# A hybrid attention and Mamba-2 layer on one core: the order of TensorE's work is written out by hand instead of left to the scheduler

## The chip, the core and the metric

The kernel runs on one core of a Trainium2 chip. The metric is the time of one execution on the device, in microseconds. The kernel is written in a tile language: the program names tiles, pools of buffers and instructions, and a scheduler puts the instructions of each engine into a queue. Each engine (TensorE or PE, VectorE or DVE, ScalarE or ACT, GpSimd or POOL, and SyncE or SP, which only starts DMAs) then runs its queue strictly in order, and waits at an instruction until its operands and its output buffer are free.

## What is computed

One decoder layer over 1024 tokens of width 1024, all in float32:

```python
h = rmsnorm(x, g_pre)
q, k, v, g_att, z, xbc, dt_raw, merge_logits = split(h @ w_in)
# branch A, 8 heads: two causal softmax maps a head, their difference
a = softmax(q0 k0' + bias) - lam * softmax(q1 k1' + bias)
o = rmsnorm(a @ v, att_subln_g) * (1 - lambda_init) * silu(g_att)
y_att = o @ w_att_proj
# branch B, 8 groups of 4 heads: Mamba-2 scan in chunks
xs, B, C = split(silu(causal_depthwise_conv(xbc)))
y = (ssd_chunked_scan(xs, softplus(dt), A, B, C) + xs * d_skip) * silu(z)
y_ssm = group_rmsnorm(y) @ w_ssm_proj
mixed = sigmoid(gate_att) * y_att + sigmoid(gate_ssm) * y_ssm
out = x + rmsnorm(mixed @ w_out, g_post)
```

## The kernel before

**Products.** Each large product is made of three: both operands are split into a high and a low part (`split`: ACT copies the high part, then DVE or POOL subtracts), and PE adds high x high, high x low and low x high (`mm3`, L144). A `proj_T` is half of a projection with transposed output: 24 matmuls of 512 columns. A `proj_N` is one block of 128 tokens: 24 matmuls of 256 columns.

**Stages.** First x is normalised and transposed into hTH and hTL. Then `attention(h)` runs for eight heads, with the projections of the merge gates (`gates`) behind each; then `branch_att` projects the attention output; then `ssm(g)` runs for eight groups, and the last four gates; then the last stage projects the ssm output (tiles pys), mixes, and makes the output projection (pout). Between stages the data go through DRAM: o_d, y_d, sig_d (gates), mix_d.

**In a head.** Projections pq, pk (two halves each) and pv (eight blocks, values and the output gate). Then, for each of eight blocks of 128 queries, `attend`: the scores s on PE; max, exponential and difference p on DVE and ACT; the transposes pta of p on PE and their split into ah and al; and the product po on PE. After four blocks, a part, comes the normalisation: ACT sums the squares of o, DVE computes the inverse root in ten small steps (`rsqrt`, `rms`), DVE scales the four tiles o, and PE transposes them (pto, L306). ACT evicts pto to oT, and a DMA writes it to o_d.

**In a group.** Projections pub, puc, pux (each with a convolution of four taps on DVE) and pz. Then, for each of eight chunks of 128 tokens, `prepare` (transposes px and a product on PE, several steps on ACT, DVE and POOL that make xb, xe, xdt, v, mt) and `advance` (the products pd on PE, the state st, the output v). After four chunks, a part, `finish` normalises as in attention: Square on ACT, the small DVE steps, four scalings of v, and the transposes pty (L627), which ACT evicts to yT, and which a DMA writes to y_d.

**What sets the order.** The program writes one head after the other and one group after the other. The scheduler decides for every engine, PE among them, which instruction goes next; it can move a later projection's matmuls in front of a transpose that isn't ready. Loads are issued from SP's queue. The stores sig_d, o_d, y_d and mix_d, the copies of kh and kl and the loads of mt are issued from ACT's queue. The low parts of the weights are made by DVE, except those of the gates and of the first head, which POOL makes.

**Buffers.** PSUM has three pools of two buffers: projections (`psp`), scores and pd (`pss`), and all else (`pst`: pta, po, pto, px, pty). The weights of one `proj_T` have two buffers.

## Time and profile before

| | |
|---|---|
| three runs | 1926.62, 1930.2, 1932.01 us; median 1930.2 |
| profiled execution | 1931.15 us, of which the span is 1929.4 us |
| granted TensorE clock over the span | 0.989 |
| PE busy | 1828.1 us (95%) |
| DVE, ACT, POOL busy | 1183.5, 862.4, 136.3 us |
| stages by their PE work | head to 52 us, attention to 712, its projection to 850, ssm to 1621, gates to 1641, last stage to the end |

A row of the timeline gives start, length, engine, line and names; in brackets stands the idle time of the engine before it and what ended that. A row of windows gives for each engine its busy time and, in parentheses, its instructions, then the granted clock of TensorE (PEclk, 1.00 is full speed), the share of the DMA engines and their rate. A row of the wait table gives the waiting instruction, what released it, the total, the number of waits, and the longest.

### The profile page before, as it was taken

The numbers are of one execution on the slowest core, as the hardware profiler recorded it, in microseconds if no ns is written. First come the engines' busy times: TensorE is split into PE (matmuls) and PEld (weight loads), VectorE is DVE, ScalarE is ACT, GpSimd is POOL, SyncE is SP. The second block draws the span as 40 slices with busy tenths as digits, with TensorE's granted clock in tenths as the row PEclk, the third lists the DMA queues.
The fourth block names the chain that finished last, engine by engine and source line by source line (L and its number), as shares of the span: only waits on it lengthen the run. The fifth ranks groups of instructions, "written<-read, shape, count | busy, mean of one in ns | idle before, by whom it ended". The sixth has DMA issues, their size and how long they took to land. (4 is left out here: it accounts for less than half of the span.)

```text
span 1929.4 us, 27946 instructions
## 1 busy us (share of the span) xinstructions
PE 1828.1 (95%) x10249; PEld 1564.5 (81%) x10249; DVE 1183.5 (61%) x2782; ACT 862.4 (45%) x2135; POOL 136.3 (7%) x154
## 2 busy tenths in 40 slices
PE   6999999999999999999899989998989999999998
PEld 4888889789888878888787878787878777877786
DVE  5576486766757553247576767676757676545433
ACT  6455364545636442125445444545444545332221
POOL 1000000000000010001010101010101022000000
PEclk9999999999999999999999999999999999999999
DMA  6121222222122135513222222222222225653532
GB/s 204 55 75 56 53 58 59 70 61 60 54 54 66 37 125 178 166 34 79 70 61 72 63 69 63 70 65 71 63 64 64 69 50 173 220 172 134 175 110 71
DMA packets 222279, 169.34 MB, mean 88 GB/s; under 512 B 12733, under 2 KB 187167, under 8 KB 222143
## 3 DMA queue, kind: packets, MB, share of 16 engines
q1 hardware_dynamic: 169390, 117.21, 20.7%
q10 hardware_dynamic: 52752, 50.36, 9.0%
q8 instruction: 81, 1.33, 0.3%
q14 instruction: 56, 0.45, 0.1%
HBM read 129.63 MB, written 31.08 MB: 83 GB/s over the span
## 5 line engine op out<-in xcount | busy, mean ns | idle before, releaser
L150 PE MATMUL pz<-wzh,hTL 128*128 128x256 f32 (+1 forms) x512 | 152.0, 297 | 0.0
L150 PE MATMUL pz<-wzh,hTH 128*128 128x256 f32 (+1 forms) x512 | 149.6, 292 | 0.3 <-DVE dtr L539 0.3
L150 PE MATMUL pz<-wzl,hTH 128*128 128x256 f32 (+1 forms) x512 | 148.0, 289 | 0.0
L150 PE MATMUL pv<-wvh,hTH 128*128 128x256 f32 x512 | 144.5, 282 | 0.7 <-DVE kl L277 0.4
L150 PE MATMUL pv<-wvl,hTH 128*128 128x256 f32 x512 | 144.8, 283 | 0.0
L150 PE MATMUL pv<-wvh,hTL 128*128 128x256 f32 x512 | 144.0, 281 | 0.0
L586 ACT ACTIVATE mt<-mt,acs 128x128 f32<-128x128 f32 x256 | 85.6, 391 | 112.9 <-DMA mt<-arow_d 112.9
L580 POOL TENSOR_TENSOR v<-xb,dsk 128x256 f32<-128x256 f32 x64 | 51.1, 808 | 683.6 <-ACT xb L572 613.6
L331 DVE TENSOR_REDUCE ng<-s 128x2 f32<-128x1024 f32 (+2 forms) x96 | 91.3, 952 | 12.4 <-PE s L323 11.9
L150 PEld LDWEIGHTS pv<-wvh,hTH 128*128 128x128 f32 x512 | 97.0, 190 | 2.3 <-PE pv L150 0.5
L150 PEld LDWEIGHTS pz<-wzh,hTH 128*128 128x128 f32 x512 | 97.7, 191 | 1.5 <-PE pz L150 0.5
L150 PEld LDWEIGHTS pz<-wzl,hTH 128*128 128x128 f32 x512 | 97.6, 191 | 0.5
L150 PEld LDWEIGHTS pz<-wzh,hTL 128*128 128x128 f32 x512 | 97.1, 190 | 0.7
L150 PEld LDWEIGHTS pv<-wvl,hTH 128*128 128x128 f32 x512 | 96.7, 189 | 0.3
L150 PEld LDWEIGHTS pv<-wvh,hTL 128*128 128x128 f32 x512 | 96.2, 188 | 0.0
L342 ACT ACTIVATE p<-s,ngm 128x512 f32<-128x512 f32 (+3 forms) x128 | 76.7, 610 | 34.9 <-DVE ngm L337 34.8
L513 DVE SCALAR_TENSOR_TENSOR xT<-ux,cw,xT 128x512 f32<-128x512 f32 x96 | 75.7, 789 | 20.2 <-ACT xT L511 18.8
L607 PE MATMUL pd<-xdt,mt 128*128 128x64 f32 x512 | 66.6, 273 | 11.0 <-DVE st L605 4.8
L607 PEld LDWEIGHTS pd<-xdt,mt 128*128 128x128 f32 x512 | 62.4, 191 | 16.4 <-ACT mt L586 9.0
L366 PE MATMUL po<-vv,ah 128*128 128x256 f32 x288 | 74.8, 289 | 0.0
L289 DVE TENSOR_TENSOR vv<-pv,vv 128x128 fp32r<-128x128 f32 x64 | 18.6, 291 | 87.8 <-ACT vv L288 87.6
L367 PE MATMUL po<-vv,al 128*128 128x256 f32 x288 | 71.8, 282 | 0.0
(869 smaller groups left out, 5423.0 us busy)
## 6 DMA issues: line engine op xcount, KB each, us to landing
mt<-arow_d ACTq DMA_DIRECT2D x64, 256.0 KB, 4.9
sig_d<-gt ACTq DMA_DIRECT2D x32, 256.0 KB, 2.1
y_d<-yT ACTq DMA_DIRECT2D x32, 256.0 KB, 2.1
yT_l<-y_d SPq DMA_DIRECT2D x32, 256.0 KB, 5.7
xt<-in_x SPq DMA_DIRECT2D x8, 512.0 KB, 5.8
kh<-kh ACTq DMA_DIRECT2D x32, 128.0 KB, 2.3
kl<-kl ACTq DMA_DIRECT2D x32, 128.0 KB, 2.3
o_d<-oT ACTq DMA_DIRECT2D x16, 256.0 KB, 2.0
```

Of the source, the lines that this page charges most:

```text
L150: nc.tensor.matmul(ps, a, b, start=(i == 0), stop=(i == n - 1))
L289: nc.vector.tensor_tensor(vv[:, t, DV:], ps[:, 0:DV], f32(vv[:, t, 0:DV]), op=ALU.subtract)
L331: nc.vector.tensor_reduce(ng, s[:, :, 0:width], axis=AX.X, op=ALU.max, negate=True)
L342: nc.scalar.activation(p[:, m, lo:lo + width], s[:, m, 0:width], AF.Exp, bias=neg[:, m:m + 1], accum_out=sums[:, i, m:m + 1])
L366: nc.tensor.matmul(po[:, 0:256], ah[:, k, :], vv[:, k, :], start=(k == 0), stop=False)
L367: nc.tensor.matmul(po[:, 0:256], al[:, k, :], vv[:, k, :], start=False, stop=(k == qb))
L513: nc.vector.scalar_tensor_tensor(out_h, u[:, j:j + 512], cw[:, j, ct:ct + 1], out_h, op0=ALU.mult, op1=ALU.add)
L580: nc.gpsimd.tensor_tensor(v4(v), v4(xb[:, 0:256]), b4(dsk[:, hs]), op=ALU.mult)
L586: nc.scalar.activation(mt[:, i, :], mt[:, i, :], AF.Relu, scale=-1.0, bias=acs[:, c, g * HG + i:g * HG + i + 1])
L607: nc.tensor.matmul(pd[:, 0, i * PH:(i + 1) * PH], mt[:, i, :], xdt[:, i * PH:(i + 1) * PH], start=True, stop=True)
```

## The change

**PE's order is the program's.** From the first stage's transposes on, PE is scheduled by hand: its instructions run in the order in which the program writes them. The other engines are still ordered by the scheduler.

**A stream of projections.** A class `Stream` holds a list of jobs, each with a function that loads weights and a generator that yields after each piece: half a `proj_T` (12 matmuls) or a `proj_N` (24). `advance` runs the stream to the next yield, `take(n)` runs a number of steps that may be fractional, and carries the rest over; `finish(n)` runs all to job n. When a job starts, the weights of the next are loaded. In attention the stream holds the projections of the next head and a gate or more; in ssm those of the next group.

**Consumers in lagged stages.** A block's work is cut into `scores`, `weights` (the pta transposes) and `output` (po), and the loop runs the scores of one block between the weights and the output of the block before:

```diff
+                    due()
+                    if before:
+                        before.weights()
+                        stream.take(0.2 * n)
+                    block.scores()
+                    stream.take(0.3 * n if before else 0.5 * n)
+                    if before:
+                        before.output()
+                        if j == 0:
+                            normed(*ended)
+                    stream.take(0.5 * n)
+                    before = block
```

`normed` makes the normalisation and puts the transposes pto into a list `later`; `due()` at the next block's start emits them. In ssm a chunk's px is made two chunks ahead of its pd, and the load of mt three ahead; `finish` puts pty into `later` in the same way:

```diff
+            due()
+            state = chunk(i).advance(state if c else None)
+            if c % 4 == 3:
+                finish(g, c // 4, [chunk(i - 3 + j) for j in range(4)], squares[g, c // 4])
+            stream.take(0.4 * steps / NT)
+            if i + 3 < len(chunks):
+                chunk(i + 3).load()
+            if i + 2 < len(chunks):
+                if c == 6 and g + 1 < SG:
+                    stream.finish(start + 4)
+                chunk(i + 2).prepare()
+            stream.take(0.6 * steps / NT)
```

The last four gates run in the last group's chunks instead of behind them. In attention one gate goes with each of heads 0 to 5, none with head 6 and four with head 7, and two come behind.

**What moves between engines.** The low parts of the weights of attention, gates, attention projection and ssm are made by POOL; in the last stage every second split is. All DMAs that were issued from ACT's queue are issued from SP's.

```diff
-        load_cols(w_in, 0, OZ + g * 256, 256, "", f"wz{g}", wh=wh, wl=wl, eng=nc.vector)
+            load_cols(w_in, 0, OZ + g * 256, 256, "", f"wz{g}", wh=wh, wl=wl, eng=nc.gpsimd)
...
-            nc.scalar.dma_start(o_d[h, :, part * 512:part * 512 + 512], oT)
+            nc.sync.dma_start(o_d[h, :, part * 512:part * 512 + 512], oT)
...
-                nc.scalar.dma_start(y_d[ct, :, part * 512:part * 512 + 512], yT)
+                nc.sync.dma_start(y_d[ct, :, part * 512:part * 512 + 512], yT)
...
+                split(wh[:, k0:k0 + 4, :], wl[:, k0:k0 + 4, :], raw, nc.gpsimd if k0 else nc.vector)
...
+                split(th, tl, f32(tl), nc.gpsimd if i % 2 else nc.vector)
```

**Buffers.** kh, kl, vv and gg have two buffers instead of one, oT one instead of two, v 10 instead of 7, mt 4 instead of 3, xb, xdt and xe 3 instead of 2, the tiles of x 6 instead of 8, and the last stage's weights 4 instead of 2. In `advance` the product of cT and the state is now the last of a pd instead of the first.

PE runs the same matmuls, tile by tile. DVE's queue has 2527 rows instead of 2735, ACT's 1676 instead of 1884, POOL's 385 instead of 159 and SP's 675 instead of 452.

**The order at three places.** The first is PE's queue where the first head ends and the second begins: po_7 is the product of the head's last block, pto_1 its second part's transposes, pk and w_1 belong to the next head. Before:

```order
L366 MATMUL po_7_1116<-vv_326,ah_7_1098 128x256
L367 MATMUL po_7_1116<-vv_326,al_7_1099 128x256
L150 MATMUL pk_1_1349<-hTL,w_1h 128x512
L150 MATMUL pk_1_1349<-hTH,w_1l 128x512
L150 MATMUL pk_1_1349<-hTH,w_1h 128x512
...
L306 MATMUL pto_1_1152<-cst,o_4_938 128x128
L150 MATMUL pk_1_1349<-hTH,w_1h 128x512
L306 MATMUL pto_1_1152<-cst,o_5_1000 128x128
```

And now, where pta_0 and s_0 are the next head's first block:

```order
L484 MATMUL po_7_1649<-vv_97,ah_7_4_1590 128x256
L485 MATMUL po_7_1649<-vv_97,al_7_4_1591 128x256
L502 MATMUL pto_1_1689<-cst,o_4_1233 128x128
L502 MATMUL pto_1_1689<-cst,o_5_1414 128x128
L502 MATMUL pto_1_1689<-cst,o_6_1539 128x128
L502 MATMUL pto_1_1689<-cst,o_7_1666 128x128
L475 MATMUL pta_0_0_1699<-cst,p_0_0_1607 128x128
L153 MATMUL pk_0_1636<-hTH,wk2h 128x512
```

The 17 matmuls of pk that stood between po_7 and pto_1 are gone from there; twelve of pk stand in front of po_7 now, and twelve behind pta_0. The same rows stand at seven of the eight heads.

The second place is ACT's queue at the end of a head's first part: the copy of po_3 (sq_3), the Square of o_3 that completes the sums sso, the evictions vv and gg of the projection pv, and the eviction of pto. Before (wvh, w_2h are weight splits and gt is a gate):

```order
L370 ACTIVATE sq_3_1779<-po_3_1769,rec_3_1755 128x128
L98 ACTIVATE wvh_2309<-wg2r_0_2319 128x4x128
L372 ACTIVATE sq_3_1779,sso_0_1640<-o_3_1778 128x128
L98 ACTIVATE w_2h<-w_2r_0_2177 128x512
L396 ACTIVATE gt_1_2154<-pg_1_2129 128x512
...
L308 ACTIVATE oT_0_1806<-pto_0_1797,subg 128x512
```

And now:

```order
L488 ACTIVATE sq_3_1088<-po_3_1078,rec_3_935 128x128
L315 ACTIVATE vv_713<-pv_1_1110 128x128
L490 ACTIVATE sq_3_1088,sso_0_715<-o_3_1087 128x128
L317 ACTIVATE gg_714<-pv_1_1110 128x128
L504 ACTIVATE oT_0_1144<-pto_0_1139,subg 128x512
```

The eviction of pv_1 has moved in front of the Square. On PE pv_1 stands directly behind po_3, and pto_0 directly behind pv_1.

The third is PE's queue at the end of ssm, where pg are gates, pty_1 the last group's second part, and pys the first product of the last stage. Before:

```order
L627 MATMUL pty_1_0_16138<-cst,v_7_16077 128x128
L627 MATMUL pty_1_1_16146<-cst,v_7_16077 128x128
L150 MATMUL pg_0_16296<-hTL,wm14h 128x512
L150 MATMUL pg_0_16296<-hTH,wm14l 128x512
...
L150 MATMUL pg_1_16390<-hTH,wm15l 128x512
L150 MATMUL pys_0_16533<-yT_h_16445,wp_0_0h 128x512
```

And now:

```order
L796 MATMUL pd_7_16381<-st_6_16338,cT_14913 128x256
L153 MATMUL pg_1_16412<-hTH,wm15h 128x512
...
L817 MATMUL pty_1_0_16440<-cst,v_7_16310 128x128
L817 MATMUL pty_1_1_16448<-cst,v_4_16065 128x128
...
L153 MATMUL pys_0_16593<-yT_h_16485,wp_0_0h 128x512
L153 MATMUL pys_0_16593<-yT_l_16486,wp_0_0h 128x512
```

Before, 86 gate matmuls stood between the last pty and the first pys; now all gates stand in front of the last pty. In SP's queue the two stores y_d from this pty now stand ahead of the first three loads of w_ssm and of the sixteen loads yT_l.

More of the change, by code (lines that the diff above doesn't have):

```diff
@@ L200, in load_x @@
+    head = Head(0)
+    with tc.tile_pool(name="norm", bufs=1, reuse_waits="tile") as work:
         def load_x(half):
@@ L376, in load_rhs @@
[L376 to L383 removed]
+                first.append(load_cols(w_in, 0, OQ, P, "wa", "wq0", eng=nc.gpsimd))
+            for _ in head.keys(first[0], half):
+                pass
@@ new lines, in tile_hybrid_layer @@
+    with tc.tile_pool(name="attn", bufs=2, reuse_waits="tile") as work:
+        stream.finish(1)
+        before = None
+        shares = [2.0 + 0.7 * (qb + 1) for qb in range(NT)]
+        for h in range(HEADS):
+            steps = 0
+            if h + 1 < HEADS:
+                following = Head(h + 1)
+                add_head(following)
+                steps += 16
+            else:
+                following = None
+            for _ in range(1 if h < 6 else 0 if h == 6 else 4):
+                add_gate(next(gate_next))
+                steps += 4
+            for part in range(2):
+                ss = small.tile([P, 4], F32, tag="ss4", name=f"sso{h}_{part}")
+                blocks = [Block(head, part * 4 + j, ss[:, j:j + 1]) for j in range(4)]
+                for j, block in enumerate(blocks):
+                    n = steps * shares[part * 4 + j] / sum(shares)
+                    due()
[10 more added lines that the diff above has]
+                    before = block
+                ended = (head, part, blocks, ss)
+            if following:
+                following.load_near()
+                stream.finish(len(stream.jobs))
+                head = following
+        for _ in range(2):
+            add_gate(next(gate_next))
+        stream.finish(len(stream.jobs) - 2)
+        before.weights()
+        stream.take(2)
+        before.output()
+        normed(*ended)
+        stream.take(3)
+        while later:
+            due()
+        stream.take(1)
@@ L399, in branch_att, with att_steps, steps @@
[L399 to L405 removed]
+        def att_steps(d):
+            def steps(w, half):
                 sl = slice(half * 512, half * 512 + 512)
```

781 lines of the change are left out of this document (467 added, 314 removed).

## The prediction

> **What bounds the kernel now.** I read the page's busy line first, then the busy time by stage, then TensorE's waits, then the timeline around those waits.
>
> ```profile
> span 1929.4 us, 27946 instructions
> PE 1828.1 (95%) x10249; PEld 1564.5 (81%) x10249; DVE 1183.5 (61%) x2782; ACT 862.4 (45%) x2135; POOL 136.3 (7%) x154
> ```
>
> PE is the bound, and 1929.4 - 1828.1 = 101 us of the span it does nothing. The change removes no matmul, so what it can move is these 101 us and the slow clock that follows a pause. By stage (head 0 to 52 us, attention 52 to 712, ssm 850 to 1621, the last gates, the first output half):
>
> ```profile
> core 0: us, PE busy (x) PEld busy (x) DVE busy (x) ACT busy (x) POOL busy (x), PEclk, DMA share, GB/s
> 52.00:712.00 660.00, 644.75 (x4010) 564.31 (x4009) 432.40 (x1098) 327.15 (x969) 26.29 (x21) 0.99 0.21 60
> 850.00:1621.00 771.00, 722.27 (x4170) 623.41 (x4170) 540.29 (x1268) 381.78 (x896) 97.26 (x120) 0.99 0.25 67
> 1621.00:1641.00 20.00, 20.00 (x88) 16.22 (x87) 9.65 (x15) 12.03 (x21) 0.00 (x0) 1.00 0.88 279
> 1641.00:1745.00 104.00, 95.89 (x408) 76.68 (x406) 53.38 (x84) 41.04 (x70) 0.00 (x0) 0.98 0.65 208
> ```
>
> PE idles 771 - 722.27 = 48.7 us in the ssm stage, 660 - 644.75 = 15.3 us in attention, 104 - 95.89 = 8.1 us where the output projection begins. The wait table (total, times, longest) names the waits: transposes that come at the end of a normalisation, and the small products of a chunk.
>
> ```profile
> PE pty L627 <- DVE v L623: 19.3, 11, 2.8
> PE pto L306 <- DVE o L305: 11.6, 9, 2.6
> PE px L566 <- ACT yT L630: 10.6, 7, 2.0
> PE pout L150 <- ACT mixH L682: 3.9, 1, 3.9
> ```
>
> A pause costs more than itself. These are the longest pto wait, two pty waits (the idle time stands in brackets), and the windows behind such pauses; the PEclk column is the granted clock.
>
> ```profile
> 215.15 0.30 PE L306 MATMUL pto<-cst,o 128*128 128x128 f32 x1 [2.57 <-DVE o L305]
> 948.74 1.61 PE L627 MATMUL pty<-cst,v 128*128 128x128 f32 x8 [2.76 <-DVE v L623]
> 1619.76 1.13 PE L627 MATMUL pty<-cst,v 128*128 128x128 f32 x8 [2.07 <-DVE v L623]
> 215.00:219.00 4.00, 3.85 (x12) 3.08 (x13) 0.79 (x4) 0.69 (x1) 0.00 (x0) 0.57 0.13 51
> 949.00:953.00 4.00, 4.00 (x16) 3.31 (x15) 0.38 (x2) 1.52 (x3) 0.00 (x0) 0.57 0.32 119
> 1526.00:1530.00 4.00, 4.00 (x15) 3.28 (x13) 0.24 (x1) 1.38 (x3) 0.00 (x0) 0.57 0.35 131
> 1620.00:1624.00 4.00, 4.00 (x23) 3.28 (x22) 0.40 (x2) 1.27 (x2) 0.00 (x0) 1.00 0.74 216
> ```
>
> After 2.57 and 2.76 us of waiting the clock is 0.57 for 4 us, which loses 4.00 x 0.43 = 1.72 us; after 2.07 us it stays 1.00. The same dip stands three times in attention (from 215, 379 and 543 us) and five times in ssm (the first and the last are quoted).
>
> [...]
>
> **The change part by part.** *Head boundaries in attention.* The new order puts pto of a head's second part directly behind its po_7, at 7 of the 8 heads; between them nothing is left for PE. The chain it then waits for is in the trace at the last head, where DVE and ACT were free (start, length):
>
> ```profile
> 703.39 0.28 PE L367 MATMUL po<-vv,al 128*128 128x256 f32 x1
> 703.72 0.37 ACT L370 ACTIVATE sq<-po,rec 128x128 f32<-128x128 f32 x1 [2.01 <-PE po L367]
> 704.12 0.35 DVE L371 SCALAR_TENSOR_TENSOR o<-po,rec,sq 128x128 f32<-128x128 f32 x1 [1.69 <-ACT sq L370]
> 704.50 0.31 ACT L372 ACTIVATE sq<-o 128x128 f32<-128x128 f32 x1 [0.42 <-DVE o L371]
> 704.94 0.17 DVE L115 TENSOR_SCALAR rsv_o<-sso 128x4 f32<-128x4 f32 x1 [0.47 <-ACT sq L372]
> 706.92 0.16 DVE L109 SCALAR_TENSOR_TENSOR rsy_o<-rst_o,rsy_o 128x4 f32<-128x4 f32 x1
> 707.12 1.14 DVE L305 SCALAR_TENSOR_TENSOR o<-o,rsy_o,gg 128x128 f32<-128x128 f32 x4
> 707.61 0.50 PE L306 MATMUL pto<-cst,o 128*128 128x128 f32 x2 [0.23 <-DVE o L305]
> ```
>
> From the end of po (703.67) to pto is 3.94 us, so 7 x 3.94 = **27.6 us**. Before, PE filled this chain with key projections. The next head's pta_0 stands behind the waiting pto, and its projections behind that.
>
> *The first part of a head.* Here one tile pv_1 of 24 matmuls stands between po_3 and pto in six heads:
>
> ```profile
> 62.95 0.28 PE L150 MATMUL pv<-wvh,hTH 128*128 128x256 f32 x1
> 65.80 0.28 PE L150 MATMUL pv<-wvh,hTH 128*128 128x256 f32 x1
> L288 ACT ACTIVATE vv<-pv 128x128 fp32r<-128x128 f32 x64 | 17.8, 278 | 107.1 <-PE pv L150 101.6 <-DVE kl L277 2.1 <-DVE s L328 2.0
> ```
>
> It is 65.80 - 62.95 = 2.85 us long and would hide most of the chain. But ACT's queue has the eviction of pv_1 ahead of the Square that the chain needs (the order in the section on the change), so the chain's second half begins only when pv_1 is done: 0.28 us of eviction, then 707.61 - 704.50 = 3.11 us from the Square to pto, 3.39 us of wait. Six heads give 20.3 us. In the last two heads half a projection (12 matmuls of 512 columns; 24 take 1626.77 - 1621.19 = 5.58 us, so 2.79 us) covers without such a hold: 2 x (3.94 - 2.79) = 2.3 us. Together **22.6 us**.
>
> ```profile
> 1621.19 0.39 PE L150 MATMUL pg<-hTH,wm14h 128*128 128x512 f32 x1
> 1626.77 0.39 PE L150 MATMUL pg<-hTH,wm14h 128*128 128x512 f32 x1
> ```
>
> *Slow clock behind them.* All 7 + 6 long pauses are over 2.57 us: 13 x 1.72 = **22.4 us**.
>
> *Weight splits on POOL.* The low parts of the weights of attention, gates and ssm move from DVE to POOL, and POOL's instruction rows go from some 154 to 385. What one does to a DVE operation that meets it:
>
> ```profile
> 209.58 1.31 POOL L99 TENSOR_TENSOR wm2l<-wm2r,wm2h 128x512 fp32r<-128x512 f32 x1 [77.55 <-DVE rst_o L107]
> 209.76 1.15 DVE L109 SCALAR_TENSOR_TENSOR rsy_o<-rst_o,rsy_o 128x4 f32<-128x4 f32 x1
> ```
>
> A step of 0.16 us took 1.15 us and ended with POOL's 1.31. Sixteen chains in attention could each lose a whole one: 0 to 16 x 1.0 us. Ten such instructions in a head of 82 us (660/8) meet a 4 us chain with a chance of 10 x (4 + 1.3) / 82 = 0.65 and then cost half of 1.3 us on average: 16 x 0.65 x 0.65 = 7 us. [...]
>
> What goes in attention: the 15.3 us of idle time and three dips, 15.3 + 5.2 = 20.4 us. Attention: 27.6 + 22.6 + 22.4 + 7 - 20.4 = **+59**. Bounds: +30 (no dip, no block) to +68 (all sixteen blocked).
>
> *The ssm stage.* pd of a chunk comes two chunks behind its px, with four half projections (4 x 2.79 = 11.2 us) or pz tiles between them, cover enough for px and pd waits of at most 2.0. pty of the second part has three pz tiles (3 x 2.85 = 8.55 us) in front of it. Before, 16 matmuls of pz and 15 of pub (16 x 0.119 + 15 x 0.232 = 5.4 us, from the same two intervals) stood there and the wait reached 2.8: a chain of up to 8.2 us, which now just fits. So the 48.7 us of idle time and 5 x 1.72 = 8.6 us of dips go; I keep 6 us for blocks by POOL: **-51**, bounds -60 and -35.
>
> *The moved DMAs and the output's start.* The gates' matmuls no longer stand behind the last pty: pys follows it directly, and in SP's queue y_d, weights and yT loads follow each other. The cover before was the 20.00 us of PE work from 1621 to 1641. The chain:
>
> ```profile
> L630 ACT ACTIVATE yT<-pty,cg 128x512 f32<-128x512 f32 x32 | 20.1, 678 | 9.9 <-PE pty L627 9.9
> yT_l<-y_d SPq DMA_DIRECT2D x32, 256.0 KB, 5.7
> L98 ACT ACTIVATE yT_h<-yT_l 128x512 fp32r<-128x512 f32 x32 | 19.1, 626 | 8.3 <-DMA yT_l<-y_d 6.2 <-PE pys L150 1.5 <-ACT gt L396 0.4
> L99 DVE TENSOR_TENSOR yT_l<-yT_l,yT_h 128x512 fp32r<-128x512 f32 x32 | 20.8, 689 | 12.8 <-ACT yT_h L98 12.8
> ```
>
> Two evictions 1.4, the loads' landing 5.7, the split 0.63 + 0.69 = 8.4, and about 2 us of queue for the two y_d and three weight loads ahead (an estimate from the 5.7: they share the same engines) give 10.4 us, with a dip 12.1. Against this, four buffers for the weights instead of two take away what isn't pout's: 8.1 - 3.9 = 4.2, and a dip, 5.9. Net **+6**, bounds 0 to +15. Between attention and its output projection only o_d is queued ahead of three loads, behind 36 gate matmuls (1.5 x 5.58 = 8.4 us): **+1**, 0 to 8. In the head the second half of x waits in SP behind weights that POOL releases: **+2**, -2 to +8.
>
> Sum: +59 - 51 + 6 + 1 + 2 = **+17**. The profiled execution took 1931.15 us, 1.75 more than its span and 0.95 more than the median of 1930.2. 1931.15 + 17 = 1948; against the median 1947.
>
> **The rivals.** *No slow clock behind the pauses (faster).* If the clock holds through pauses of 3.4 to 3.9 us, at the 13 pto places and before pys, 22.4 + 1.7 us go from the sum: 1947 - 24 = **1923**. It decides from the point where fewer than 4 of the 13 pauses are followed by a clock of 0.57 (ten dips of 1.72 are the 17 us of the sum). For it: only pauses up to 2.76 us were seen in these stages, and the 2.07 us one brought no dip. Against it: every window quoted behind a longer one shows 0.57. [...]
>
> *Small products cost less when they are not cut up (faster).* PE's busy time holds hidden losses too. In ssm 8 groups of 8 x 2.85 + 8 x 5.58 = 67.4 us of projections make 539 of 722 us, with some 25 us of gates; about 158 us are small products, which before stand in runs of one to three between projections. Attention has as much: 644.75 less 8 x 56.3 (four halves of 5.58, eight tiles of 2.85, one gate of 11.2) less 45 for four more gates is 150. If unbroken runs take a tenth off, 31 us go: **1916**. For it: px, pd and pty now stand in whole pieces. Against it: nothing in the trace shows a price for the cut itself.
>
> *DVE and POOL become the bound in ssm (slower).* Before, DVE is busy 540 and POOL 97 us there. 96 weight splits move: DVE loses 96 x 0.69 = 66, POOL gains 96 x 1.31 = 126, together 540 - 66 + 97 + 126 = 697 of 720 us. If most of these exclude each other, chunks fall behind and the gain of 51 shrinks to about 20: **1978**. It decides where the two together exceed the stage. Against it: operations that read PSUM needn't be blocked, and the rows show one DVE step blocked, not all.
>
> **How the numbers follow.** Forecast 0.50 (1947; its own range 1925 to 1964), no slow clock 0.15, cheaper small products 0.20, DVE and POOL 0.15. The range reaches from 1902, below the second rival, to 1976, near the third. A measurement of this kernel can tell about 0.3% from no change, so 1924.4 to 1936 is the same. The forecast gives slower 0.38, same 0.08, faster 0.04; the first rival faster 0.11, same 0.03, slower 0.01; the second faster 0.18, same 0.02; the third slower 0.15. Sums: faster 0.33, same 0.13, slower 0.54.
>
> **What would show it right or wrong.** Right: the wait table names pto <- DVE o with about 50 us in 15 places, the longest near 4; the clock dips behind them, twice a head; idle time in ssm under 10 us; and a wait of some 10 us of pys for its first yT. The first term is wrong if pto waits are short at head boundaries; the second if pto of the first part waits about 1 us; the third if PEclk holds 1.00 behind them. The forecast's sign is wrong if attention's total comes out under +42 us while ssm gives back 51 or more. If DVE steps of 0.2 us show 1.2 us all through ssm and pty or pd wait for them, the third rival holds.

## The result, and the profile after

The changed kernel takes **2202.6 us** (median of four runs, 2201.3 to 2207.6), the kernel before 1931.1 us (median of four as well). The ratio is **1.141**, with a 95% interval of 1.137 to 1.145. The forecast was 1947 us in a range of 1902 to 1976: its direction held, its size didn't, by 256 us. The profiled execution took 2207.63 us, its span is 2205.8 us.

The busy line of the page after:

```profile
span 2205.8 us, 27992 instructions
PE 1930.1 (87%) x10249; PEld 1643.9 (75%) x10249; DVE 1156.1 (52%) x2556; ACT 863.8 (39%) x2135; POOL 445.9 (20%) x380
```

PE runs the same 10249 matmuls, but is busy 102 us longer and idle 2205.8 - 1930.1 = 276 us instead of 101. The longer busy time is the clock, whose mean over the span is 0.936 (0.989 before): busy time times clock is 1930.1 x 0.936 = 1807 us, and 1828.1 x 0.989 = 1808 us before. The table goes by stage, with boundaries put where the attention projection (pya) and the last stage (pys) begin on PE. PE makes the same matmuls in each stage in both kernels, so the last column is the slower clock:

| | before | after | difference | of it PE idle | of it PE busy |
|---|---|---|---|---|---|
| start to the first pya | 734.4 | 844.8 | +110.4 | +77.3 | +33.1 |
| first pya to the first pys (its projection, ssm, last gates) | 906.3 | 1064.0 | +157.7 | +91.7 | +66.0 |
| first pys to the end | 288.7 | 297.0 | +8.3 | +5.4 | +2.9 |

The windows of attention, ssm and the last stage after:

```profile
core 0: us, PE busy (x) PEld busy (x) DVE busy (x) ACT busy (x) POOL busy (x), PEclk, DMA share, GB/s
84.00:845.00 761.00, 672.05 (x3905) 586.06 (x3904) 411.00 (x1030) 328.89 (x964) 101.22 (x78) 0.95 0.20 55
935.00:1900.00 965.00, 835.15 (x4457) 713.10 (x4455) 564.49 (x1202) 387.73 (x911) 225.23 (x210) 0.92 0.21 55
1909.00:2205.00 296.00, 273.29 (x1152) 220.07 (x1152) 130.81 (x230) 85.93 (x156) 77.11 (x55) 0.96 0.48 154
```

DVE is busy 564 of 965 us in ssm, and PE idles 130 us there. Neither engine is full, so something makes one wait for the other. The wait table of PE names it:

```profile
PE pd L793 <- DVE st L791: 111.8, 48, 6.3
PE pto L502 <- DVE o L497: 65.4, 15, 6.9
PE pta L475 <- DVE p L465: 22.1, 18, 2.1
PE pout L153 <- ACT mixH L941: 10.1, 1, 10.1
...
PE pys L153 <- ACT yT_h L97: 8.7, 1, 8.7
...
PE pd L793 <- DVE st L788: 5.7, 8, 2.0
...
PE pty L817 <- DVE v L811: 3.7, 2, 2.8
```

The pty and px waits of before (19.3 and 10.6 us) are nearly gone, as forecast. The first row is new: 48 + 8 waits, one for each chunk that makes a new state, 117.5 us in all. One of them on the timeline:

```profile
1200.42 0.59 PE L785 MATMUL pd<-xe,xb 128*128 128x256 f32 x2
1202.28 2.33 DVE L724 SCALAR_TENSOR_TENSOR xT<-ux,cw,xT 128x512 f32<-128x512 f32 x3 [0.50 <-ACT xT L722]
1204.53 0.42 DVE L791 TENSOR_TENSOR st<-pd,st 128x256 f32<-128x256 f32 x1
1205.00 1.93 PE L793 MATMUL pd<-xdt,mt 128*128 128x64 f32 x8 [3.98 <-DVE st L791]
1206.72 1.17 PE L796 MATMUL pd<-st,cT 128*128 128x256 f32 x2
1206.00:1210.00 4.00, 4.00 (x13) 3.34 (x13) 1.67 (x5) 0.31 (x1) 0.61 (x1) 0.50 0.16 41
```

PE makes the product of xb and xe (L785, done at 1201.0). DVE must read it out of the tile pd to make the new state st (L791), but three conv steps of the next group stand ahead of that in DVE's queue. PE's next instruction, L793, writes another part of the same tile pd. It waits 3.98 us until DVE has read, and starts 0.05 us after DVE's end. The window behind it runs at 0.50 of the clock. In the kernel before the same pieces stood on PE like this:

```profile
1009.37 0.65 PE L597 MATMUL pd<-st,cT 128*128 128x256 f32 x2
1009.86 0.59 PE L599 MATMUL pd<-xe,xb 128*128 128x256 f32 x2
...
1013.05 1.08 PE L607 MATMUL pd<-xdt,mt 128*128 128x64 f32 x8 [0.58 <-DVE st L605]
1013.96 0.65 PE L597 MATMUL pd<-st,cT 128*128 128x256 f32 x2
```

L599 is the product of xb and xe, and the L607 at 1013.05 is the product with mt of the same chunk, 2.6 us behind its end. Between them PE made two px matmuls and 15 of pz, and it waited only 0.58 us for the same read by DVE. In the whole kernel before there are 56 such stretches, of 1.1 to 5.1 us (median 2.2), which the scheduler had mostly filled with other chunks' and projections' matmuls. They add up to 135 us; the written order puts the two products back to back and leaves this time open.

In attention the forecast waits are there. The first pto after a first part, a head boundary, and the first part of the seventh head:

```profile
128.83 1.26 PE L502 MATMUL pto<-cst,o 128*128 128x128 f32 x4 [4.39 <-DVE o L497]
181.92 1.17 PE L502 MATMUL pto<-cst,o 128*128 128x128 f32 x4 [3.94 <-DVE o L497]
699.54 1.17 PE L502 MATMUL pto<-cst,o 128*128 128x128 f32 x4 [6.91 <-DVE o L497]
182.00:186.00 4.00, 4.00 (x12) 3.23 (x13) 0.85 (x4) 0.86 (x2) 0.00 (x0) 0.50 0.17 66
```

### The profile page after: what moved, and what is told of

Same layout as the page of the kernel before. It is cut to its first block, busy times and chain, and to the rows that moved or that the text cites. A ratio compares the mean times of both kernels' runs of the same rounds, so it can differ in the third digit from the quotient of the medians.

```text
span 2205.8 us, 27992 instructions
## 1 busy us (share of the span) xinstructions
PE 1930.1 (87%) x10249; PEld 1643.9 (75%) x10249; DVE 1156.1 (52%) x2556; ACT 863.8 (39%) x2135; POOL 445.9 (20%) x380
## 4 chain that ended last, share of the span: by engine, by line
PE 25%; DMA 12%; DVE 8%; ACT 6%; issue 4%; POOL 1%; SPq 0%; DVEq 0%; POOLq 0%; ACTq 0%
DMA mt<-arow_d 8%; PE pz L153 7%; PE pys L153 4%; PE pout L153 4%; PE pd L793 3%; DVE xT L724 2%; PE pux L153 2%; ACT mt L775 2%; PE pd L796 1%; PE pg L153 1%; DMA wor<-in_w_out 1%; DMA yT_l<-y_d 1%; DVE bT L724 1%; PE puc L153 1%; DVE cT L724 1%
## 5 line engine op out<-in xcount | busy, mean ns | idle before, releaser
L793 PE MATMUL pd<-xdt,mt 128*128 128x64 f32 x512 | 87.3, 325 | 117.5 <-DVE st L791 111.8
L793 PEld LDWEIGHTS pd<-xdt,mt 128*128 128x128 f32 x512 | 78.1, 233 | 140.6 <-DVE st L791 131.6
L153 PE MATMUL pz<-wzh,hTH 128*128 128x256 f32 (+1 forms) x512 | 154.6, 302 | 3.5 <-DVE dtr L705 2.0
L153 PE MATMUL pv<-wvh,hTH 128*128 128x256 f32 x512 | 149.1, 291 | 0.4 <-DVE qs L300 0.4
L724 DVE SCALAR_TENSOR_TENSOR xT<-ux,cw,xT 128x512 f32<-128x512 f32 x96 | 86.8, 904 | 37.9 <-ACT xT L722 37.0
L153 PEld LDWEIGHTS pv<-wvh,hTH 128*128 128x128 f32 x512 | 102.3, 200 | 0.7 <-PE pv L153 0.6
L804 ACT ACTIVATE sqy<-v 128x256 f32<-128x256 f32 x64 | 26.6, 416 | 190.5 <-DVE v L802 190.5
L98 DVE TENSOR_TENSOR al<-pta,ah 128x512 fp32r<-128x512 f32 (+2 forms) x96 | 52.0, 555 | 71.7 <-ACT ah L97 71.6
L502 PE MATMUL pto<-cst,o 128*128 128x128 f32 x64 | 18.7, 441 | 65.4 <-DVE o L497 65.4
```

What stands on the lines that cost most here:

```text
L98: (eng or nc.vector).tensor_tensor(l, src, f32(h), op=ALU.subtract)
L153: nc.tensor.matmul(ps, a, b, start=(i == 0), stop=(i == n - 1))
L502: nc.tensor.transpose(pt[:, j * P:(j + 1) * P], b.o, ident)
L724: nc.vector.scalar_tensor_tensor(out_h, u[:, j:j + 512], cw3[:, j, ct:ct + 1], out_h, op0=ALU.mult, op1=ALU.add)
L793: nc.tensor.matmul(pd[:, 0, i * PH:(i + 1) * PH], mt[:, i, :], self.xdt[:, i * PH:(i + 1) * PH], start=True, stop=True)
L804: nc.scalar.activation(sq, v, AF.Square, accum_out=self.ss)
```

## The experiments

Theory A, formed from the rows above: the cost is waits that a written order leaves uncovered, above all the product L793 behind L785 and pto behind its chain, with the half clock that follows. Rival B: the loads of mt come late, because they now stand in SP's queue behind weights. Rival D: POOL's splits slow DVE down, and DVE is behind. The time before was 1930 to 1937 us beside these runs. A time with no range is one execution, and it is the profiled one; the times after are compared with 2203 us.

**Two ways to take the wait in a chunk away.** The first undoes the order of the products:

```diff
             new = None
+            for i in range(HG):
+                nc.tensor.matmul(pd[:, 0, i * PH:(i + 1) * PH], mt[:, i, :], self.xdt[:, i * PH:(i + 1) * PH],
+                                 start=True, stop=True)
+            if c > 0:
+                nc.tensor.matmul(pd[:, 1, 0:256], g.cT[:, tok], state, start=True, stop=True)
             if c < NT - 1:
                 nc.tensor.matmul(pd[:, 1, 256:512], self.xb[:, 256:384], self.xe, start=True, stop=True)
...
-            for i in range(HG):
-                nc.tensor.matmul(pd[:, 0, i * PH:(i + 1) * PH], mt[:, i, :], self.xdt[:, i * PH:(i + 1) * PH],
-                                 start=True, stop=True)
-            if c > 0:
-                nc.tensor.matmul(pd[:, 1, 0:256], g.cT[:, tok], state, start=True, stop=True)
```

> One part undone in ssm: within a chunk's pd, TensorE first makes the four products with mt, then the product of cT and the state, and last the product of xb and xe, from which DVE makes the new state st. Theory A (the products with mt wait because they stand behind the product that DVE must first read out of the same tile pd, and DVE has conv steps queued ahead of that read): the 117 us of pd <- DVE st fall under 15, the half clock that follows these waits goes too (the granted clock of the stage was 0.91, so up to 81 us), and the time is near 2203 - 112 - 60 = 2030 us, between 2000 and 2060. Rival B (mt itself comes late, because its load stands in SP's queue behind loads of weights): the wait stays and only changes its name, and the time is 2150 to 2200.

Measured: 2122.9 us, between A's range and B's. The wait pd <- DVE st is gone. But a new one is there, pty <- DVE v, 78.1 us in 8 waits of up to 11.3.

The second keeps PE's order and gives the product a PSUM tile of its own:

```diff
+                ps = pst.tile([P, 512], F32, tag="t", name=f"ps{nm}")
-                nc.tensor.matmul(pd[:, 1, 256:512], self.xb[:, 256:384], self.xe, start=True, stop=True)
+                nc.tensor.matmul(ps[:, 0:256], self.xb[:, 256:384], self.xe, start=True, stop=True)
```

> TensorE's order stays as in the changed kernel, but the product of xb and xe goes to a PSUM tile of its own, so that the products with mt behind it need not wait until DVE has read it. Theory A: the same effect as with the other order, within 20 us of it (2000 to 2060), with pd <- DVE st under 15 us; some new waits for the third kind of tile in a pool of two buffers are possible (up to 15 us). If instead the order of the products matters and not the shared tile: no gain, 2190 to 2210. Rival B as before: 2150 to 2200.

Measured: 2118.9 us. The two agree within 4 us, so it is the shared tile that makes L793 wait and not the order of the products as such. That settles the mechanism. Its price was only partly right: 80 and 84 us instead of about 170. A good part of the rest came back at once in its wait table:

```profile
PE pto L502 <- DVE o L497: 65.4, 15, 6.9
PE pty L818 <- DVE v L812: 53.1, 9, 8.1
```

The stall in each chunk had covered this wait. Without it PE arrives earlier at pty, the first transposes after a part's fourth chunk, and their chain on DVE and ACT isn't done. A part of that is DVE's conv steps, which take longer than before, beside POOL's splits:

```profile
1254.98 1.49 POOL L98 TENSOR_TENSOR wx13l<-wx13r,wx13h 128x512 fp32r<-128x512 f32 x1 [0.20 <-ACT wx13h L97]
1256.09 4.33 DVE L724 SCALAR_TENSOR_TENSOR cT<-uc,cw,cT 128x512 f32<-128x512 f32 x3 [0.77 <-ACT cT L722]
1256.65 1.52 POOL L98 TENSOR_TENSOR wx13l<-wx13r,wx13h 128x512 fp32r<-128x512 f32 x1 [0.18 <-ACT wx13h L97]
1258.28 1.59 POOL L98 TENSOR_TENSOR wzl<-wz3r,wzh 128x512 fp32r<-128x512 f32 x1
```

Three conv steps take 4.33 us where they took 2.33 in the stretch shown above. Another part comes after them, within the 6.48 us of PE's wait:

```profile
1266.08 0.40 ACT L775 ACTIVATE mt<-mt,acs 128x128 f32<-128x128 f32 x1 [2.13 <-DMA mt<-arow_d]
1266.99 0.17 DVE L717 COPY ux<-ux 128x3 f32<-128x3 f32 x1 [2.05 <-ACT ux L721]
1270.36 1.26 PE L818 MATMUL pty<-cst,v 128*128 128x128 f32 x4 [6.48 <-DVE v L812]
```

The rest of the small steps of the normalisation stands in DVE's queue behind a copy that needs ACT's eviction of ux. That eviction stands in ACT's queue behind an instruction that waits for the load of mt. So DVE is idle for 2.05 us here, and for 1.5 to 3.1 us in six of these nine waits: it isn't only DVE's work that makes pty late.

**The moved DMAs (rival B).** Copies of kh and kl, loads of mt, and the stores sig_d, o_d, y_d and mix_d are issued from ACT's queue again:

```diff
-            nc.sync.dma_start(self.mt, bass.AP(arow_d.tensor, ...
+            nc.scalar.dma_start(self.mt, bass.AP(arow_d.tensor, ...
```

> One part of the change undone alone: all the DMAs that moved from ACT's queue to SP's (copies of kh and kl, loads of mt, stores sig_d, o_d, y_d, mix_d) are issued from ACT again. Theory A says that the large wait (pd <- DVE st) has nothing to do with mt's load, so it stays at 100 to 125 us and the time within 15 us of 2203. Rival B (mt comes late because its load stands in SP's queue behind the loads of weights): the wait falls by half or more, and the time is under 2150.

Measured: 2190.9 us, and pd <- DVE st is 110.5 us in 48 waits. B falls as the cause of this wait. The one execution is 12 us below the median of the change; its stretch from pya to pys is 17 us shorter, 4 of them at pys, which waits 4.6 us for yT_h instead of 8.7. That ACT itself waits for the load of mt is another matter; it comes back below.

**The transposes pto, one block later.**

```diff
-        later.append([1, transposed])
+        later.append([2, transposed])
```

> Attention alone: the transposes pto are emitted one block later, so that two half projections and a product po, or two tiles pv, lie between the end of their chain's input and them. Theory A (the waits at pto are uncovered chains, and half clock follows each): the 65 us in 15 waits fall under 8, and 13 to 15 dips of about 1.7 us go: 2203 - 57 - 24 = 2122, between 2105 and 2140. Rival C (the wait at pto also covered what stands behind it, so that pta waits in its place): pta's 22 us grow by 20 to 40 and the time is 2145 to 2180.

Measured: 2138.2 us, at the upper end of A's range. pto falls from 65.4 to 4.3 us, and pta rises from 22.1 to 41.4 in 26 waits: A holds, and C holds beside it with 19 us. The attention projection begins at 780.6 us instead of 844.8, 64 us earlier: 65.4 - 4.3 - (41.4 - 22.1) = 42 us of waits, and some 22 us that are left for the clock. PE's busy time up to pya says the same: 709.4 us instead of 733.4, 24 less for the same matmuls.

**Pause or clock?** Twelve unread matmuls are put in front of pto at the seven head boundaries:

```diff
+                pf = psp.tile([P, 512], F32, tag="pp", name=f"pfill{h}")
+                for i in range(12):
+                    nc.tensor.matmul(pf, hTH[:, 0, 0:P], hTH[:, 0, 0:512], start=(i == 0), stop=(i == 11))
```

> Twelve matmuls of 512 columns whose result nobody reads are put directly in front of pto at the seven head boundaries (2.79 us each, 19.5 us of added work). This separates the pause from the half clock behind it. If half clock follows only pauses of over about 2.5 us: the seven waits of 3.93 shrink to about 1.1, the clock behind them stays 1.00, and the time falls by 7 x 1.7 = 12 us although work was added (2191, that is 2186 to 2197). If the dips cost nothing by themselves: the time stays within 3 us of 2203. If the fill delays what follows: 2206 or more.

Measured: 2199.0 us (2195.4 to 2201.8, four runs), a ratio to the kernel before of 1.139 (1.134 to 1.143). The intervals overlap with the change's, so this is no gain that can be told, where 12 us were expected. The windows show why. First the changed kernel, at the second boundary and behind the next pause:

```profile
280.22 1.17 PE L502 MATMUL pto<-cst,o 128*128 128x128 f32 x4 [3.93 <-DVE o L497]
290.90 0.30 PE L475 MATMUL pta<-cst,p 128*128 128x128 f32 x1 [2.10 <-DVE p L465]
280.50:284.50 4.00, 4.00 (x15) 3.19 (x15) 0.66 (x3) 0.86 (x2) 0.00 (x0) 0.63 0.17 66
290.50:294.50 4.00, 3.60 (x18) 3.12 (x19) 2.24 (x4) 1.00 (x4) 0.00 (x0) 1.00 0.00 0
```

And the kernel with the fill:

```profile
277.79 1.02 PE L506 MATMUL pto<-cst,o 128*128 128x128 f32 x4 [1.20 <-DVE o L497]
287.29 0.49 PE L475 MATMUL pta<-cst,p 128*128 128x128 f32 x2 [2.08 <-DVE p L465]
278.00:282.00 4.00, 4.00 (x21) 3.23 (x21) 0.72 (x3) 1.12 (x3) 0.00 (x0) 1.00 0.17 66
287.50:291.50 4.00, 4.00 (x14) 3.47 (x13) 2.08 (x3) 0.99 (x4) 0.00 (x0) 0.58 0.00 0
```

The fill removes the dip behind pto, as expected (0.63 becomes 1.00). But the pause of 2.08 us at the next pta has a dip behind it now (0.58), where a pause of 2.10 us has none in the changed kernel (1.00). It is the same from the second boundary to the fifth: the dip has moved and not gone. At the first boundary the changed kernel has both dips, and with the fill one is left; at the last two the dip goes. So three dips of seven go, and the 19.5 us of added work stand against 65.4 - 46.2 = 19.2 us less of waiting at pto. What is left is within the spread of the runs.

**Both lags.** The tile of its own, pto and pty each one stage later:

```diff
-        later.append([1, transposed])     (in normed, attention)
+        later.append([2, transposed])
...
-        later.append([1, transposed])     (in finish, ssm)
+        later.append([2, transposed])
```

> The tile of its own for the product of xb and xe (2119 us), and both kinds of lagged transposes one stage later: pto by one block more, pty by one chunk more. Theory A (what is left are transposes whose chain is longer than the cover that the written order gives): the 65 us of pto fall under 8 and the 53 us of pty under 10, with the dips behind them; pto's part gave 64 us in its own run, pty's gives 45 plus 8 dips of 1.7: 2119 - 64 - 58 = 1997, between 1980 and 2015. Rival D (DVE, slowed by POOL's splits, is behind TensorE in ssm, and the wait only moves to the next product that needs DVE): over 2030, with waits of 30 us or more at pd, ps, px or pz.

Measured: 2020.9 us, just above A's range and below D's. pto waits 4.3 us, pty for DVE's v no longer stands in the table; instead pty <- DVE cbm has 15.0 us (its second tile waits for the buffer that px holds), and pux <- ACT xT 21.3 in 6 waits. So a part of the wait did move on, but well under D's 30 us at one place, and not to DVE alone: in five of the six pux waits ACT stands idle for 1.6 to 2.2 us until the load of mt has landed, and the eviction of pux stands behind that in its queue.

**Who makes the weights' low parts (rival D).** First with both lags and DVE's splits:

```diff
-        return lambda: load_cols(w, row0, col0, P, "wa", name, eng=nc.gpsimd)
+        return lambda: load_cols(w, row0, col0, P, "wa", name)
```

(and the same for the weights of pv and pz.)

> As the run with both lags, and the low parts of the weights of attention, gates, attention projection and ssm are made by DVE again (POOL's queue has 181 rows instead of 385). Rival D: a POOL split of 1.3 to 1.6 us blocks DVE's steps (conv steps of 0.79 us were seen at 1.44 each beside it), so DVE's chains become shorter although it gets some 0.69 us of work for each split: 15 to 40 us faster than with both lags. Theory A alone: the chains are only as long as their own steps, and DVE's extra 140 us of work lie in front of them: the same to 20 us slower.

Measured: 2001.5 us, 19 us faster, as D has it. The stages differ in sign. From the first pya to the first pys it takes 902.8 us instead of 944.3, 41 us less; attention's end comes at 797.4 us instead of 778.1, 19 us later. The conv steps in ssm, by a group of each kernel (count, busy us, mean ns), with both lags and then with DVE's splits:

```profile
L724 DVE SCALAR_TENSOR_TENSOR xT<-ux,cw,xT 128x512 f32<-128x512 f32 x96 | 89.6, 933 | 27.4 <-ACT xT L722 26.7
```

```profile
L724 DVE SCALAR_TENSOR_TENSOR xT<-ux,cw,xT 128x512 f32<-128x512 f32 x96 | 72.4, 754 | 8.3 <-ACT xT L722 7.6
```

Then the same edit in the changed kernel alone:

> The changed kernel with one part undone: the low parts of the weights of attention, gates, attention projection and ssm are made by DVE again, as in the kernel before (POOL keeps those of the last stage). In the kernel before, the same part alone cost 50 us; with both lags and the tile of its own, undoing it gave 41 us in ssm and cost 19 us in attention. If a block by POOL is most of the wait pd <- DVE st: that wait falls from 112 us to under 60, and the time under 2140. If the wait is the queue order on DVE (three conv steps of 0.76 us ahead of the state's step): it stays over 90 us, and the time is 2165 to 2215.

Measured: 2172.1 us, in the range set for the queue order. pd <- DVE st falls from 111.8 to 86.2 us, which is just below the bound of 90 set for the queue order and far above the 60 for a block by POOL: the order on DVE is most of that wait. The quarter that goes is POOL's share less what DVE's added splits cost there. In exchange pty <- DVE v rises from 3.7 to 24.7 us.

And the kernel before with this one part of the change:

```diff
-            w = load_cols(w_in, 0, col, P, "wa", f"w{nm}{g}", eng=nc.vector)
+            w = load_cols(w_in, 0, col, P, "wa", f"w{nm}{g}", eng=nc.gpsimd)
```

(and the same for the weights of pq, pk, pv, pz and pya.)

> The kernel before with one part of the change alone: the low parts of the weights of attention, attention projection and ssm are made by POOL, the order of everything is the scheduler's. The prediction's third rival put a price on this: DVE and POOL together near the stage's length in ssm, up to 31 us. If blocks by POOL matter by themselves: 1940 to 1965. If DVE's relief (about 0.69 us for each of some 170 splits) outweighs them: 1915 to 1930. My estimate: 1938.

Measured: 1980.5 us (1980.4 to 1984.8, four runs), a ratio of **1.026** (1.023 to 1.030). The estimate of 1938 was far too low, and the time lies above both ranges. POOL's splits alone make the kernel 50 us slower, although DVE is relieved: 27 us up to the first pya, 24 from there to the first pys. Its busy line:

```profile
PE 1836.8 (93%) x10249; PEld 1557.8 (79%) x10249; DVE 1154.5 (58%) x2612; ACT 863.8 (44%) x2135; POOL 368.3 (19%) x324
```

DVE loses 170 instructions and only 29 us of busy time; at 0.69 us each they were 117 us, so 88 us came back as longer operations. POOL gains 232 us. PE is idle 1978.6 - 1836.8 = 142 us instead of 101.

**Versions after what the runs point to.** Products with mt first, both lags, ssm's splits on DVE and attention's on POOL, more projections beside a head's first blocks, half of the last gates behind the last chunk, and priority for the mix:

```diff
-        shares = [2.0 + 0.7 * (qb + 1) for qb in range(NT)]
+        shares = [3.5 + 0.4 * (qb + 1) for qb in range(NT)]
...
-                    steps = 4 * (len(stream.jobs) - start)
+                    steps = 8
...
-            if c == NT - 1:
+            if c == NT - 1 and g + 1 < SG:
                 stream.finish(len(stream.jobs))
+        stream.take(3)
         while later:
             due()
+        stream.finish(len(stream.jobs))
```

> A version that applies what the runs so far point to, with one idea for each stage: products with mt first in a chunk (no tile of its own), both lags of two, the low parts of the ssm weights on DVE again (attention's stay on POOL), a larger share of projections beside the first blocks of a head (3.5 + 0.4 per block instead of 2.0 + 0.7), eight of the last gates' sixteen half projections behind the last chunk as cover for pty and the loads of yT, and priority for the steps that make the mix. From the stage times of the earlier runs: attention 778 us in place of 734 before, minus about 25 of pta waits and their dips, is 753; ssm took 903 with DVE's splits, minus 12 of ps waits and 14 for the gates that now lie in front of pys, is 885; the last stage 297, minus 8 for pys that is covered and 6 for pout, is 283: 753 + 885 + 283 = 1921, between 1900 and 1950. If DVE's backlog in ssm is still there: over 1950, with pty and pz waits of 30 us and more.

Measured: 1945.8 us, inside the range and 25 above the sum: attention's end at 747.6, 899.5 us to the first pys, 296.9 us for the rest. Attention came out 5 us better than expected, the other two 28 us worse.

The same with the tile of its own, the old shares, and pto behind pta:

```diff
-                    due()
                     if before:
                         before.weights()
                         stream.take(0.2 * n)
+                    due()
```

> The same with two differences: the product of xb and xe has a tile of its own (in place of the other order in a chunk), and in attention the shares are as in the change, but the late transposes pto come behind pta of their block and not in front of it. In ssm: about 12 us slower than the run with the other order, by the waits for the third user of a pool of two buffers. In attention: if pta's 3.2 us waits at a head's second block come from the rms steps that stand ahead in DVE's queue, the place of pto on TensorE changes little (within 5 us of 778 at the start of the attention projection); if pto itself held pta up, about 760. Time: 1925 to 1965.

Measured: 1979.4 us, above the range. Attention ends at 771.3, 7 us from the 778.1 with the same shares and 24 from the 747.6 with the new ones: the place of pto matters little there, and the shares did most. From pya to pys it takes 911.1 us, 12 us more than the other order, as expected.

And the first of the two with the stores on ACT's queue, pty's tiles apart, and w_out loaded earlier:

```diff
-        later.append([2, transposed])
+        later.append([2, lambda: transposed(0)])
+        later.append([3, lambda: transposed(1)])
...
-            nc.sync.dma_start(sig_d[d, :, half * 512:half * 512 + 512], th)
+            nc.scalar.dma_start(sig_d[d, :, half * 512:half * 512 + 512], th)
```

> The version with the other order in a chunk (1946 us), with four further edits: the stores sig_d, o_d and y_d are issued from ACT's queue again (in that version SP waited from 1629 to 1640 us at the stores of the last gates, and the loads of the last stage stood behind them); the two tiles of pty come one chunk apart, because the second waited for a buffer that px holds (24 us in ten waits); w_out is loaded before the products of its block in place of after them. Expected: pys 7.8 us and 2 us of dip gone, pty 24 falls under 6, pout's 9.5 to about 5: 1946 - 10 - 18 - 4 = 1914, between 1900 and 1930. If the loads wait for space that the stage before still holds and not for SP's queue: pys still waits 5 us or more, and the time is 1920 to 1945.

Measured: 1948.5 us (1944.8 to 1950.0, six runs), a ratio of 1.009 (1.007 to 1.011): above both ranges, no faster than the 1945.8 us of the version it starts from, and still slower than the kernel before. pty's waits for px's buffer went (17 us), pys fell from 7.8 to 3.9 us, but pz <- ACT xT came with 26.1 us in 7 waits, where none stood before. One of them:

```profile
1170.68 1.28 ACT L775 ACTIVATE mt<-mt,acs 128x128 f32<-128x128 f32 x4 [3.35 <-DMA mt<-arow_d]
1172.34 0.76 ACT L722 ACTIVATE xT<-pux,cg,cw 128x512 f32<-128x512 f32 x1
1173.16 0.58 PE L153 MATMUL pz<-wzh,hTH 128*128 128x256 f32 x1 [4.45 <-ACT xT L722]
```

pz needs the PSUM buffer that pux holds until ACT has read it, and ACT stands before that for the load of mt. So it is in the five longest of the seven, 23.3 us together, in which ACT waited 1.95 to 3.35 us for mt. B's late load, which wasn't the cause of the wait in a chunk, is a part of this one; no run here gives mt another buffer or an earlier load without the shared tile, so what that would be worth stays open. In this stage a removed wait returned at the next place each time: from pd to pty, from there to pty's second tile, and from there to pz. No version here beats the kernel before.

## Why the prediction was wrong

**The step that failed is the ssm term, -51.** It said that the px and pd waits have "cover enough" and that pty's chain "just fits". For px that held: it isn't in the table. pty's chain fit by luck: it waits 3.7 us for v beside the new stall, and 53.1 us in the same order without it. For pd it was wrong. The step looked only at the distance from px to pd, which the lag of two chunks makes, and not at the instructions within pd, which the change puts back to back. L793 waits there for DVE's read of the shared tile, 117.5 us in 56 waits, for which the sum has no term. The kernel before showed the dependency, as pd L607 <- DVE st L605 with 4.8 us in 10 waits, and the scheduler hid the rest of it, in the 135 us of filled stretches.

From the first pya to the first pys it became 158 us longer: 92 us of idle time and 66 of slower clock (0.92 in the window). The forecast's sign of being right, idle time in ssm under 10 us, failed with 130. Without the 8.7 us of pys, which belong to the output's start, the stage gave +149 in place of -51, which is 200 of the 260 us between the forecast of 1948 and the profiled execution.

Both runs that take the dependency away give back 80 to 84 us at once. Run by run the stretch goes from 1064.0 us to 975.8 with the tile of its own, to 944.3 with pty one chunk later, and to 902.8 with DVE's splits: 88 us for the shared tile, 32 for pty's chain, 41 for POOL. The change and the forecast also took for granted that DVE and ACT answer in time: without the stall they don't, and even the best versions take 898 to 903 us there against 906 before. In no version tried were the 51 us to be had: DVE's and ACT's queues, the load of mt and the buffers put the waits back elsewhere.

**The head boundaries, +27.6,** were right: seven waits of 3.93 to 3.94 us, 3.94 forecast.

**The first parts, +22.6,** were under-sized: 4.39 us in six heads (3.39 forecast), and 6.91 and 4.57 in the last two (1.15 forecast), 37.8 us. The forecast took the chain from a place where DVE and ACT were free, and here they aren't. In the six heads DVE has parts of the next block's p and the second half of vv between the Square and the small steps, so that from the Square to pto it takes 4.00 us and not 3.11. In the seventh head the Square starts only at 692.16, behind the exponentials of the next block in ACT's queue, and p (2.02 us) and qs (1.38 us) stand between the small steps on DVE. In the last head two small steps of 0.16 us take 1.26 and 1.18 us beside splits of POOL:

```profile
692.16 0.32 ACT L490 ACTIVATE sq<-o 128x128 f32<-128x128 f32 x1
692.96 2.02 DVE L465 SCALAR_TENSOR_TENSOR p<-p,nlam 128x512 f32<-128x512 f32 x2
777.95 1.26 DVE L108 SCALAR_TENSOR_TENSOR rsy_o<-rst_o,rsy_o 128x4 f32<-128x4 f32 x1
```

**The half clock, +22.4 in attention,** was the right mechanism. Behind all fifteen pauses at pto the clock is 0.50 to 0.59 over the next 4 us, so nothing is left of the first rival (no slow clock). The size was too low: up to the first pya PE is busy 33.1 us longer, where 22.4 - 5.2 = 17.2 us were forecast, and ssm has 66 us, which weren't forecast. One later block for pto gave 64 us, of which 42 are waits. The fill shows that a dip per pause is too simple a count: a dip that is prevented can come at the next pause. There a pause of 2.08 us had a dip behind it (0.58), and in the changed kernel one of 2.10 us at the same place had none (1.00).

**POOL, +7 in attention and up to 31 in the third rival,** was under-sized: 50 us in the kernel before alone. The price isn't one number: with both lags, POOL's splits cost 41 us in ssm and save 19 in attention. In the rows with the tile of its own three conv steps take 1.44 us each beside POOL's splits of 1.49 to 1.59. A step that reads PSUM wasn't held up: st<-pd,st takes 0.41 to 0.43 us in all 48 places of the changed kernel, 15 of them wholly within a split of POOL, one here:

```profile
1037.52 1.68 POOL L98 TENSOR_TENSOR wzl<-wz1r,wzh 128x512 fp32r<-128x512 f32 x1 [0.66 <-ACT wzh L97]
1037.98 0.42 DVE L791 TENSOR_TENSOR st<-pd,st 128x256 f32<-128x256 f32 x1
```

The third rival was right in that POOL's work makes other steps of DVE longer; that most of the two engines' work excludes each other wasn't shown. It was given 0.15; it is a part of the result and not its main one.

**The output's start, +6,** was too low. pys waits 8.7 us (10.4 forecast), which lies in front of the first pys, and the stage behind it is 8.3 us longer, where 5.9 were to go: 17 us together, just over the upper bound of 15. pout's wait grew from 3.9 to 10.1 us, which wasn't forecast.

**The waits that the sum left at nothing** are pta's 22.1 us (2.1 before). Of attention's excess over the forecast, 110 against 59 + 1 + 2, pto is 15 us, pta 20 and the slow clock 16; less the 7 that the sum gave POOL as a term of its own, that is 44 of the 48. The second rival (cheaper small products) doesn't show: busy time times clock is 1807 us after and 1808 before.

## What to carry to other kernels

When an order is written by hand, each pair of neighbours on the bound engine is a promise that nothing lies between them: check every instruction that another engine must answer, within a stage as well as across stages, and read also the small waits of the kernel before, since they name the dependencies that the scheduler was hiding. Covering a wait gives its length only if the engine that was waited for isn't late for another reason, be it its own work or what stands ahead in its queue; so fix one, look at where the wait went, and count the gain after that. Work that is moved to an idle engine isn't free when it makes the busy one's steps longer: here the splits alone cost 50 us in the kernel before.

## What the runs showed of the hardware

The half clock depends on more than the pause before it: 2.08 us had a dip behind it in the kernel with the fill (at five head boundaries, 0.58 over 4 us at the first two), and 2.07 to 2.10 us at the same place had none in the changed kernel (1.00, at four of the five). In the changed kernel the second to the sixth head boundary come 95.5 to 95.6 us apart, two of them:

```profile
375.75 0.66 PE L502 MATMUL pto<-cst,o 128*128 128x128 f32 x2 [3.93 <-DVE o L497]
471.31 0.66 PE L502 MATMUL pto<-cst,o 128*128 128x128 f32 x2 [3.93 <-DVE o L497]
```

With the fill they come as far apart (277.79 and 373.33 us), although work was added and waits were taken away. With the tile of its own they come 95.55 to 95.63 us apart, and with pto one block later the first boundaries come 86.8 to 87.0 us apart. What sets these distances wasn't shown.

Moving 128 x 512 subtractions to POOL costs DVE more than their number suggests: each runs 1.26 to 1.83 us on POOL in the changed kernel (264 of them, median 1.30) for 0.68 to 0.69 on DVE in the kernel before, and with this one part of the change alone the mean conv step of the kernel before rises from 789 to 866 ns for xT and from 750 to 1118 ns for cT.
